# The products of c with the powers of a, on VectorE instead of GpSimd, in a two-block transformer kernel

## The chip, the cores and the metric

The kernel runs on one core of one Trainium2 chip, as one program. The metric is the device time of one execution in microseconds (us); lower is better. The times of several executions of the same program are given by their median.

## The reference

Two transformer blocks are computed on 512 tokens of width 1024, in float32. The first block has, side by side, a chunked attention of 8 heads and a state space mixer, then an attention to 256 memory tokens, then a feed-forward part that picks experts by keys (16384 experts, 8 heads, 16 picks). The second block has a dilated and a differential attention and a second part with experts. The first step of the first block is a projection of the normalised tokens to q, k, v (512 columns each) and u (512 columns).

The change lies in the state space mixer. It works on 32 groups of 16 channels, each with 64 complex states. Cut to what matters:

```
step = exp(log_step);  mag = exp(lr * step)
ar, ai = mag * cos(li * step), mag * sin(li * step)      # one complex a per state
bbr, bbi = (fr + i fi) * (br + i bi)                      # discretised input matrix
bu = einsum('blgc,gpc->blgp', u, bb)
x[l] = a * x[l-1] + bu[l]                                 # associative scan over 512 tokens
y = einsum('blgp,gcp->blgc', xr, cr) - einsum('blgp,gcp->blgc', xi, ci) + d * u
y = gelu(y);  y = y * sigmoid(y @ w_glu + b_glu)
```

## The kernel before

The kernel is a straight-line program without loops on the chip. Each engine has its own queue, which it works off strictly in order and in which it waits for the results of others. The order in a queue is not that of the source: when the program is built, a planner goes through it with estimated durations of its own, and puts next in each queue the instruction that is earliest in the source among those it takes to be ready. So the weight splits and norms of a projection (early lines) stand in VectorE's queue in between the tables of the state space mixer (later lines).

*The projections* (lines 130 to 262). The normalised tokens are transposed and split in a high and a low part, and each weight is split in the same way, so that a product needs three matmuls (mm3, lines 117 to 120). A weight of 128 rows and 512 columns is loaded by SP's queue, cast by ScalarE (L76: the high part) and subtracted by VectorE (L77: the low part). For one projection there are 8 such weights and 4 tiles of 128 tokens, 96 matmuls of 512 columns, which are summed in four PSUM tiles. ScalarE then copies each PSUM tile out (L230), which makes it free for the next projection. For q and k (head_proj, L224) ScalarE squares the copy (L235), VectorE sums the squares by heads (L236), and after the four tiles VectorE makes the inverse root (L57 to L72) and scales (L249), and TensorE transposes (L252). The tile of squares has one buffer, so square 2 waits for sum 1:

```
sq = pool.tile([128, n], F32, name="sq", tag="sq", bufs=1)
A.activation(out=sq, in_=raw[:, t, :], func=AF.Square)
V.tensor_reduce(out=ss[:, t * nh:(t + 1) * nh], in_=sq.rearrange("p (h d) -> p h d", d=hd), axis=AX.X, op=OP.add)
```

The projections come in the order q, k, u, v (L259 to L262). u is written to memory (L214), from where the mixer reads it later.

*The tables of the mixer* (lines 265 to 392). While TensorE works on the projections, VectorE makes from the parameters: a itself (L299 to L302), bbr and bbi (L341), and the powers a^0 to a^8 in par and pai by doubling (L343 to L351). GpSimd copies the powers in reverse order into rar and rai (L355, L356, 16 small copies). Then come the products of c with the powers (L358 to L371): car and cai, each 128 partitions x 16 x 9 x 16, made in two pieces (5 powers, then 4), with three instructions for each piece and each of car and cai, so twelve instructions, six of 1280 and six of 1024 elements on each of 128 partitions. One operand of the multiplications repeats each power 16 times, the other repeats c for each power. Behind them in the source VectorE makes the phase tables phc and phs (L375 to L388): squarings of 128x16 (uc, us) and products of 128x16 to 128x512, with the function cmul (L318 to L332), and dec (L390). GpSimd also clears toep (L373), which has no input and runs first of all.

*Who reads what.* rar, rai, bbr and bbi are read by the gb products (L420), the first VectorE work of the mixer after the projections; their tiles lie in memory that is free when the projections' and the tables' pools have been closed (L392 to L395). car and cai are read by TensorE in L441 and L442, after the gb products, and in L511 and L512. phc, phs and dec are read by the recurrence (L488 to L496). These stages are put in between the heads of the chunked attention (L596 on), by a list of steps written out by hand (L578).

Of the kernel before, what the change touches and what calls it, by code (L numbers as in the profile page):

```python
# [14 lines left out]
OP = mybir.AluOpType  # L15
# [8 lines left out]
def build(tc, I, out, dbg=None, stop=None):  # L24
# [22 lines left out]
    V, A, G, T, S = nc.vector, nc.scalar, nc.gpsimd, nc.tensor, nc.sync  # L47
# [286 lines left out]
    def bc(ap, axis, n):  # L334
        sh = list(ap.shape)
        sh.insert(axis, n)
        return ap.unsqueeze(axis).broadcast_to(sh)
# [26 lines left out]
    for o, n in ((0, 5), (5, 4)):  # L364
        w_ = slice(o, o + n)
        pr_, pi_ = bc(par[:, :, w_], 3, 16), bc(pai[:, :, w_], 3, 16)
        u = st.tile([128, 16, 5, 16], F32, name="cau", tag="cau")[:, :, 0:n]
        for dst, x, y in ((car, cr, nci), (cai, nci, ncr)):
            G.tensor_tensor(out=dst[:, :, w_], in0=pr_, in1=bc(x, 2, n), op=OP.mult)
            G.tensor_tensor(out=u, in0=pi_, in1=bc(y, 2, n), op=OP.mult)  # L370
            G.tensor_tensor(out=dst[:, :, w_], in0=dst[:, :, w_], in1=u, op=OP.add)  # L371
    toep = b1.tile([128, 32, 128], F32, name="toep")
    G.memset(toep, 0.0)  # L373

# [5 lines left out]
    for lvl in range(9):  # L380
        if lvl >= 3:
            n = 1 << (lvl - 3)
# [371 lines left out]
    for h2 in range(2):  # L754
        if h2 == 1:
            ws = keep_w(wk, I["w_mem_o"], 8, 0)
        for t in range(NT):
# [3 lines left out]
            for hh in range(2):  # L761
# [10 lines left out]
                for j in range(2):  # L772
# [3 lines left out]
                            in1=zs.unsqueeze(2).broadcast_to([128, 2, 256]), op=OP.mult)  # L776
# [1102 lines left out]
```

## Time and profile before

| | |
|---|---|
| runs | 3839.08, 3841.64, 3839.0 us; median 3839.08 |
| profiled execution, its own time | 3833.36 us |
| its span in the profile | 3831.6 us |
| mean granted clock of TensorE | 0.981 |
| busy: TensorE, VectorE, ScalarE, GpSimd | 96%, 78%, 43%, 47% of the span |
| chain that ended last: TensorE, VectorE | 71%, 15% of the span |

The profile is that of one execution. Its views give, among others, the busy time of each engine in any stretch, the instructions of each engine in order of time, and who waited for whom. An instruction's row in the view in order of time has its start and its duration in us, the engine (PE is TensorE, DVE is VectorE, ACT is ScalarE, POOL is GpSimd), the line of the source, the operation, the tiles out<-in, the shapes, and in brackets the idle time of the engine before it with what ended that. A duration may reach a little into the next instruction's, since the engine takes the next one while the last results are being written. Spans on GpSimd are rough.

### The profile page before, as it was taken

The numbers are of one execution on the slowest core, as the hardware profiler recorded it, in microseconds if no ns is written. First come the engines' busy times: TensorE is split into PE (matmuls) and PEld (weight loads), VectorE is DVE, ScalarE is ACT, GpSimd is POOL, SyncE is SP. The second block draws the span as 40 slices with busy tenths as digits, with TensorE's granted clock in tenths as the row PEclk, the third lists the DMA queues.
The fourth block names the chain that finished last, engine by engine and source line by source line (L and its number), as shares of the span: only waits on it lengthen the run. The fifth ranks groups of instructions, "written<-read, shape, count | busy, mean of one in ns | idle before, by whom it ended". The sixth has DMA issues, their size and how long they took to land.

```text
span 3831.6 us, 53218 instructions
## 1 busy us (share of the span) xinstructions
PE 3659.9 (96%) x19062; PEld 3158.1 (82%) x19062; DVE 2999.7 (78%) x5554; ACT 1653.4 (43%) x2567; POOL 1802.3 (47%) x1192
## 2 busy tenths in 40 slices
PE   6999999899999999999899999999899999999999
PEld 4767788788899999987777777788888899999987
DVE  8556469996898988878746577689996898888875
ACT  3554433375333333333344588333474333333333
POOL 3000037613778787760324100247424778877740
PEclk8999999999999999999999999999999999999999
DMA  3423132257899999988322333332358999999884
GB/s 111 106 95 121 55 120 88 79 207 263 318 337 321 315 325 326 326 304 281 106 72 69 90 95 103 119 107 82 111 224 269 327 338 327 319 316 325 306 284 147
DMA packets 333515, 789.04 MB, mean 206 GB/s; under 512 B 32433, under 2 KB 152321, under 8 KB 329857
## 3 DMA queue, kind: packets, MB, share of 16 engines
q1 hardware_dynamic: 259520, 517.17, 40.8%
q0 software_dynamic: 73728, 268.47, 19.3%
q8 instruction: 150, 2.46, 0.3%
q14 instruction: 117, 0.95, 0.1%
HBM read 725.34 MB, written 59.01 MB: 205 GB/s over the span
## 4 chain that ended last, share of the span: by engine, by line
PE 71%; DVE 15%; DMA 5%; ACT 4%; issue 3%; POOL 2%; SPq 1%; DVEq 0%; POOLq 0%; ACTq 0%
PE y L1305 8%; PE y L1307 8%; PE y L1306 8%; PE pa L1114 7%; PE pa L1112 7%; PE pa L1111 7%; PE pgg L1213 4%; PE mm L119 3%; PE mm L120 3%; PE mm L118 3%; DVE E L968 2%; ACT stg L1214 2%; PE mt L1603 1%; PE mt L1601 1%; DVE eq L959 1%
## 5 line engine op out<-in xcount | busy, mean ns | idle before, releaser
L1104 POOL TENSOR_TENSOR ul<-ur,uh 128x1024 fp32r<-128x1024 f32 x256 | 695.5, 2717 | 435.6 <-PE pa L1114 261.1
L1111 PE MATMUL pa<-phi,uh 128*128 128x384 f32 x2048 | 698.7, 341 | 0.9 <-ACT ga L1116 0.9
L1112 PE MATMUL pa<-plo,uh 128*128 128x384 f32 x2048 | 696.0, 340 | 0.0
L1305 PE MATMUL y<-vh,wh 128*128 128x512 f32 x1536 | 596.0, 393 | 15.0 <-ACT wh L1274 13.6
L1306 PE MATMUL y<-vl,wh 128*128 128x512 f32 x1536 | 600.4, 392 | 3.6 <-DVE vl L1276 3.5
L1307 PE MATMUL y<-vh,wl 128*128 128x512 f32 x1536 | 601.8, 393 | 2.1 <-DVE wl L1277 2.1
L1276 DVE TENSOR_TENSOR vl<-vr,vh 128x1024 fp32r<-128x1024 f32 x256 | 361.3, 1411 | 215.3 <-ACT vh L1275 215.1
L1274 ACT CAST wh<-w 128x384 fp32r<-128x384 f32 x256 | 131.5, 514 | 755.0 <-PE y L1306 547.7
L1251 DVE SCALAR_TENSOR_TENSOR acc<-vrow,act,acc 128x1024 f32<-128x1024 f32 x256 | 408.9, 1597 | 56.2 <-DMA vrow<-in_peer_v_dram,ei 28.4
L1240 DVE SCALAR_TENSOR_TENSOR urow<-urow,hgat 128x1024 f32<-128x1024 f32 x256 | 408.9, 1604 | 30.4 <-DMA urow<-in_peer_u_dram,ei 15.6
L1114 PE MATMUL pa<-phi,ul 128*128 128x384 f32 x2048 | 403.1, 340 | 15.9 <-POOL ul L1104 15.8
L1098 ACT CAST uh<-ur 128x1024 fp32r<-128x1024 f32 x256 | 269.6, 1053 | 325.4 <-issue 212.6
L1111 PEld LDWEIGHTS pa<-phi,uh 128*128 128x128 f32 x2048 | 389.5, 190 | 9.6 <-ACT ga L1116 1.2
L1112 PEld LDWEIGHTS pa<-plo,uh 128*128 128x128 f32 x2048 | 389.6, 190 | 9.1
L1114 PEld LDWEIGHTS pa<-phi,ul 128*128 128x128 f32 x2048 | 362.4, 190 | 18.0 <-POOL ul L1104 18.0
L1305 PEld LDWEIGHTS y<-vh,wh 128*128 128x128 f32 x1536 | 289.1, 189 | 71.2 <-ACT wh L1274 14.3
L1307 PEld LDWEIGHTS y<-vh,wl 128*128 128x128 f32 x1536 | 289.2, 189 | 68.5 <-DVE wl L1277 5.3
L1306 PEld LDWEIGHTS y<-vl,wh 128*128 128x128 f32 x1536 | 289.5, 189 | 63.4 <-DVE vl L1276 7.4
L77 DVE TENSOR_TENSOR wl<-wr,wh 128x512 fp32r<-128x512 f32 (+1 forms) x276 | 177.9, 653 | 142.4 <-ACT wh L76 142.1
L1275 ACT CAST vh<-vr 128x1024 fp32r<-128x1024 f32 x256 | 267.7, 1046 | 35.6 <-DMA vr<-in_peer_v_dram 24.9
L1273 DVE TENSOR_TENSOR w<-gbuf,ga 128x384 f32<-128x384 f32 x256 | 212.0, 830 | 37.1 <-DMA gbuf<-Gd 36.0
L76 ACT CAST wh<-wr 128x512 fp32r<-128x512 f32 (+1 forms) x276 | 149.4, 550 | 209.3 <-PE mm L120 129.2
(533 smaller groups left out, 7241.0 us busy)
## 6 DMA issues: line engine op xcount, KB each, us to landing
vr<-in_peer_v_dram SPq DMA_DIRECT2D x128, 512.0 KB, 6.3
ur<-in_peer_uT_dram SPq DMA_DIRECT2D x128, 512.0 KB, 4.6
vr<-in_expert_v_dram SPq DMA_DIRECT2D x128, 512.0 KB, 6.4
ur<-in_expert_uT_dram SPq DMA_DIRECT2D x128, 512.0 KB, 4.7
gbuf<-Gd SPq DMA_DIRECT2D x64, 768.0 KB, 8.8
Gd<-stg SPq DMA_DIRECT2D x24, 1920.0 KB, 6.3
wr<-in_w_in_dram SPq DMA_DIRECT2D x104, 256.0 KB, 2.8
war<-in_w_ada_dram SPq DMA_DIRECT2D x48, 512.0 KB, 4.2
```

Source lines behind the costliest of these rows:

```text
L1098: A.copy(out=uh, in_=ua[e])
L1104: G.tensor_tensor(out=ul, in0=raw, in1=uh.bitcast(F32), op=OP.subtract)
L1111: T.matmul(pa, uh[:, k, :], hi[:, k, 0:NDT], start=(k == 0), stop=False)
L1112: T.matmul(pa, uh[:, k, :], lo[:, k, 0:NDT], start=False, stop=False)
L1114: T.matmul(pa, ul[:, k, :], hi[:, k, 0:NDT], start=False, stop=(k == 7))
L1240: V.scalar_tensor_tensor(out=row, in0=row, scalar=1.0, in1=hg_, op0=OP.mult, op1=OP.mult, accum_out=act[:, k:k + 1])
L1251: V.scalar_tensor_tensor(out=acc, in0=rows_.pop((1, k)), scalar=act[:, k:k + 1], in1=acc, op0=OP.mult, op1=OP.add)
L1275: A.copy(out=vh, in_=vr)
L1276: V.tensor_tensor(out=vl, in0=vr, in1=vh.bitcast(F32), op=OP.subtract)
L1305: T.matmul(y[t][c], wh[:, ts], vh[:, cs_], start=(e_ == 0), stop=False)
L1306: T.matmul(y[t][c], wh[:, ts], vl[:, cs_], start=False, stop=False)
L1307: T.matmul(y[t][c], wl[:, ts], vh[:, cs_], start=False, stop=(e_ == 127))
```

## The change

The three instructions in the inner loop are issued to VectorE (V) where they were issued to GpSimd (G). Nothing else in the source differs; the planner orders the queues anew.

```
     for o, n in ((0, 5), (5, 4)):
         w_ = slice(o, o + n)
         pr_, pi_ = bc(par[:, :, w_], 3, 16), bc(pai[:, :, w_], 3, 16)
         u = st.tile([128, 16, 5, 16], F32, name="cau", tag="cau")[:, :, 0:n]
         for dst, x, y in ((car, cr, nci), (cai, nci, ncr)):
-            G.tensor_tensor(out=dst[:, :, w_], in0=pr_, in1=bc(x, 2, n), op=OP.mult)
-            G.tensor_tensor(out=u, in0=pi_, in1=bc(y, 2, n), op=OP.mult)
-            G.tensor_tensor(out=dst[:, :, w_], in0=dst[:, :, w_], in1=u, op=OP.add)
+            V.tensor_tensor(out=dst[:, :, w_], in0=pr_, in1=bc(x, 2, n), op=OP.mult)
+            V.tensor_tensor(out=u, in0=pi_, in1=bc(y, 2, n), op=OP.mult)
+            V.tensor_tensor(out=dst[:, :, w_], in0=dst[:, :, w_], in1=u, op=OP.add)
     toep = b1.tile([128, 32, 128], F32, name="toep")
     G.memset(toep, 0.0)
```

## Rows read from the trace of the kernel before

**Rows 1.** The page, part 1: busy time of each engine.
```profile
PE 3659.9 (96%) x19062; PEld 3158.1 (82%) x19062; DVE 2999.7 (78%) x5554; ACT 1653.4 (43%) x2567; POOL 1802.3 (47%) x1192
```
**Rows 2.** Two stretches: length, PE, PEld, DVE, ACT, POOL busy (instructions), clock, DMA, GB/s.
```profile
45.00:80.00 35.00, 12.69 (x43) 9.55 (x43) 34.73 (x75) 6.68 (x12) 23.36 (x11) 0.67 0.10 26
81.00:116.00 35.00, 34.37 (x159) 28.22 (x158) 22.50 (x55) 14.94 (x26) 0.00 (x0) 1.00 0.29 83
```
**Rows 3.** Waits from 43 to 77 us: in total, times, longest.
```profile
ACT sq L235 <- DVE ssh L236: 24.6, 3, 13.9
...
PE mm L118 <- ACT hraw L230: 17.4, 2, 11.6
```
**Rows 4.** ScalarE in order of time: squares 1 and 2 of q.
```profile
40.35 0.63 ACT L235 ACTIVATE sq<-hraw 128x512 f32<-128x512 f32 x1
...
55.57 0.63 ACT L235 ACTIVATE sq<-hraw 128x512 f32<-128x512 f32 x1 [13.89 <-DVE ssh L236]
```
**Rows 5.** TensorE in order of time: the instructions behind its long idle pieces.
```profile
56.73 0.80 PE L118 MATMUL mm<-wh,hThi 128*128 128x512 f32 x1 [11.60 <-ACT hraw L230]
...
64.21 0.79 PE L118 MATMUL mm<-wh,hThi 128*128 128x512 f32 x1 [5.83 <-ACT hraw L230]
...
76.01 1.94 PE L252 MATMUL ptq<-ident,hraw 128*128 128x128 f32 x8 [4.28 <-issue]
```
**Rows 6.** VectorE in order of time, 43 to 69 us.
```profile
43.08 2.26 DVE L331 TENSOR_TENSOR cm<-uc,us 128x16 f32<-128x16 f32 x1
45.26 0.16 DVE L327 TENSOR_TENSOR uc<-uc 128x16 f32<-128x16 f32 x1
45.37 2.33 DVE L332 TENSOR_TENSOR us<-us,cm 128x16 f32<-128x16 f32 x1
...
54.81 0.67 DVE L236 TENSOR_REDUCE ssh<-sq 128x8 f32<-128x512 f32 x1
...
66.31 2.42 DVE L327 TENSOR_TENSOR phc<-phc,uc 128x32 f32<-128x32 f32 x1
```
**Rows 7.** GpSimd in order of time: the first of the twelve products, and the third.
```profile
35.70 2.39 POOL L369 TENSOR_TENSOR car<-par,ssm_cr 128x1280 f32<-128x1280 f32 x1
...
45.27 2.40 POOL L369 TENSOR_TENSOR cai<-par,nci 128x1280 f32<-128x1280 f32 x1
```
**Rows 8.** The stretch with eleven of the products: GpSimd busy, then VectorE busy.
```profile
42.80:68.80 26.00, 25.56 (x12) 0.67 0.03 10
...
42.80:68.80 26.00, 25.76 (x27) 0.67 0.03 10
```
**Rows 9.** VectorE by line and form: count, busy us, mean ns, idle before.
```profile
L328 DVE TENSOR_TENSOR cm<-gin,phs 128x1024 f32<-128x1024 f32 x1 | 1.2, 1218 | 0.0
...
L328 DVE TENSOR_TENSOR cm<-rai,bbi 128x512 f32<-128x512 f32 x2 | 1.4, 688 | 0.0
```
**Rows 10.** VectorE in order of time: a split, and sums 1 and 2 of k.
```profile
37.62 1.03 DVE L77 TENSOR_TENSOR wl<-wr,wh 128x512 fp32r<-128x512 f32 x1 [1.85 <-ACT wh L76]
...
92.26 0.69 DVE L236 TENSOR_REDUCE ssh<-sq 128x8 f32<-128x512 f32 x1
93.71 0.69 DVE L236 TENSOR_REDUCE ssh<-sq 128x8 f32<-128x512 f32 x1 [0.76 <-ACT sq L235]
```
**Rows 11.** VectorE in order of time: the last phase table product, the first gb product.
```profile
91.57 0.68 DVE L332 TENSOR_TENSOR phs<-phs,cm 128x512 f32<-128x512 f32 x1
...
125.56 0.69 DVE L327 TENSOR_TENSOR gb<-rar,bbr 128x512 f32<-128x512 f32 x1 [1.32 <-DMA ud<-ut]
```
**Rows 12.** Two longer stretches, columns as in rows 2.
```profile
35.00:143.00 108.00, 84.77 (x369) 68.42 (x368) 75.64 (x170) 37.69 (x66) 31.55 (x23) 0.89 0.29 87
...
143.00:200.00 57.00, 50.90 (x308) 37.49 (x307) 30.07 (x87) 30.70 (x78) 0.58 (x4) 0.88 0.37 77
```
**Rows 13.** In order of time: three copies on GpSimd, a split on VectorE.
```profile
41.84 1.08 POOL L356 COPY rai<-pai 128x16 f32<-128x16 f32 x3
...
41.84 0.68 DVE L77 TENSOR_TENSOR wl<-wr,wh 128x512 fp32r<-128x512 f32 x1
```

More of the change, by code (lines that the diff above doesn't have):

```diff
@@ L368, in build @@
         for dst, x, y in ((car, cr, nci), (cai, nci, ncr)):
-            G.tensor_tensor(out=dst[:, :, w_], in0=pr_, in1=bc(x, 2, n), op=OP.mult)
-            G.tensor_tensor(out=u, in0=pi_, in1=bc(y, 2, n), op=OP.mult)
-            G.tensor_tensor(out=dst[:, :, w_], in0=dst[:, :, w_], in1=u, op=OP.add)
+            V.tensor_tensor(out=dst[:, :, w_], in0=pr_, in1=bc(x, 2, n), op=OP.mult)
+            V.tensor_tensor(out=u, in0=pi_, in1=bc(y, 2, n), op=OP.mult)
+            V.tensor_tensor(out=dst[:, :, w_], in0=dst[:, :, w_], in1=u, op=OP.add)
     toep = b1.tile([128, 32, 128], F32, name="toep")
```

## The prediction

> **What bounds the kernel now.** I read the page first, then the same 35 us of two neighbouring projections with the busy time of each engine, then the waits in the bad one, then the engines' instructions in order of time.
>
> The page says that TensorE is busy for 3659.9 us, 96% of the span [rows 1]. So only a stretch in which TensorE stands still can give much, and the products of c sit in one, near the start. From 45 to 80 us TensorE runs 43 matmuls; from 81 to 116 us, in work of the same kind, 159 in the same 35 us [rows 2]. Its granted clock is 0.67 in the first stretch, a mix of the two levels of 1.2 and 2.4 GHz, and 1.00 in the second. GpSimd is busy for 23.36 us of the first and not at all in the second.
>
> The waits name the chain [rows 3]: TensorE waits 17.4 us in two pieces for ScalarE's copies of the finished q tiles (L230), which free the PSUM tiles for the k projection; ScalarE waits 24.6 us for VectorE's sums of squares (L236), since the tile of squares has one buffer. On ScalarE, square 2 starts at 55.57 after 13.89 us of idling and only then comes copy 3 [rows 4]. TensorE's own long idle pieces are 11.60, 5.83 and 4.28 us, 21.7 us together [rows 5].
>
> Why are the sums late? VectorE stands in front of them with phase table products of 128x16 elements. Such an instruction takes 0.16 us when nothing is in its way; from 43.08 us on eleven of them take some 2 us each, the first 2.26 and the last (128x32) 2.42 us [rows 6]. They end where a GpSimd product ends: VectorE's 45.37 + 2.33 is 47.70, GpSimd's 45.27 + 2.40 is 47.67 [rows 6, 7]. The sum L236 reads one tensor and takes 0.67 us in the middle of this, as long as in a stretch without GpSimd (0.69) [rows 6, 10]. So the sums are late because two-input VectorE instructions ahead of them are held, not because VectorE has that much to do.
>
> **The change, part by part.**
>
> *Removed from GpSimd:* twelve products, the first at 35.70 us [rows 7] of 2.39 us, the other eleven filling 25.56 of the 26 us from 42.8 to 68.8 [rows 8]; 28 us. GpSimd then has nothing to do from 81 to 116 us [rows 2], so its own time is worth nothing. What counts is the hold that goes: in those 26 us VectorE has 25.76 us busy in 27 instructions [rows 8], of which two sums at 0.67 and 25 small ones at about 0.17 make 5.6; some 20 us is holding.
>
> *What that gives TensorE.* At the pace of the undisturbed stretch, 159 in 35 us, 43 matmuls take 9.5 us, so the stretch loses 25.5 us [rows 2]: 21.7 us of idling in the long pieces and 3.8 us in short ones and at the low clock after them. Of the 43, 16 are short transposes, in two pieces of eight of which one is shown [rows 5]. If these took no time at all, the other 27 would need 5.9 us and the loss would be 29.1 us; that is the far bound. I take 25.5, since the second stretch has transposes too.
>
> *Added to VectorE:* the twelve products. VectorE has no 128x1280 product in this trace. The bounds are the 128x1024 one (1.218 us, same type) and, on the far side, GpSimd's 2.4 us. The VectorE row is nearer, and the step from 512 elements (0.688 us, with operands broadcast in the same way) to 1024 costs 0.53 us, so 1280 should take 1.48 us [rows 9]. Six at 1.22 and six at 1.48 make 16.2 us. At 2.4 us each for the long ones it would be 21.7 us.
>
> *What of it lies on the path.* The products come earlier in the program than the phase tables (L380 on) and later than the projections' sums and splits. They now take the place in VectorE's queue that held phase table work had: a sum that becomes ready can stand behind a product in progress, at most 1.48 us. TensorE needs two of the four q sums: sum 1 releases copy 3, sum 2 copy 4. In the undisturbed projection sums follow one another at 1.45 us [rows 10] and TensorE is busy for 34.37 of 35 us [rows 2]. So the likely cost is two products' time less some slack: between 0 and 3.0 us, of which I take 2.5, because the order is fixed before the run and will not hit the free moments. The far bound is all twelve ahead of the sums, 16.2 us. Behind a waiting sum on ScalarE stand the next copy and the next weight cast; behind those TensorE.
>
> *Before 45 us* the last q weights can be held by a product as well. VectorE stood idle for 1.85 us there, waiting for a cast [rows 10], which covers one product and costs nothing; without that cover it costs 1.2 us.
>
> *The phase tables move back.* They end at 92.25 us, with the last of their products. With 20 us of holding gone and 16.2 us added they end near 88 us. Their reader, the first gb product, starts at 125.56 behind a transfer of u [rows 11], and that moves to about 103. Cover 14 us: cost nothing. VectorE as a whole was busy 75.64 of 108 us from 35 to 143 us [rows 12]; less 20, plus 16.2 is 72 us in about 85. It is fuller, but not full.
>
> *GpSimd's copies stay* (L355, L356). Three of them took 1.08 us, while a VectorE split with two inputs beside them took 0.68 us [rows 13], no longer than 512 elements take elsewhere [rows 9]: there VectorE did not pay. Their results are read at 103 us, so I count 0. The Trainium skill, page SBUF — State Buffer, section "Who interferes with whom", says that issue order decides which of the two is blocked, and for the whole instruction. By that rule some of the products would stand behind a copy; no row here shows VectorE paying for one. At a third of 1.08 us for each of twelve products an estimate by that rule is 4.3 us more on VectorE, and 3820 if all of it were on the path.
>
> No transfer is moved, added or removed, and SP's queue keeps its order; its weight loads come earlier with TensorE.
>
> *After 81 us* TensorE hardly stops [rows 2], so what is won stays won through the projections, and the later stages hang on their results.
>
> **Sum.** 25.5 - 2.5 = 23 us. The profiled execution took 3833.36, so 3810.4 for its like; it lies 5.7 us under the median of the three runs. Against the median: 3839.08 - 23.0 = 3816.
>
> **The rivals.**
>
> *B, the products stand in front of the sums.* If the planned order puts all twelve ahead of sum 1, as they are ready at the same time, 16.2 us replace the hold: 25.5 - 16.2 = 9.3 us won, 3830. For it: the first GpSimd product started at 35.70 and the first square was done at 40.35 + 0.63 us [rows 4, 7], and several products fit between. Against it: twelve do not, and the sums are earlier in the program.
>
> *C, won and given back.* TensorE arrives at the attention stage 23 us sooner and waits there for the recurrence's tables or for transfers that do not move. Under 7.7 us would be left, so 3832 to 3840. For it: TensorE already has gaps there, 6.1 us of the 57 after 143 [rows 12]. Against it: the tables have 14 us of cover and the transfers of u start from TensorE's results.
>
> *D, slower: the late sums have another cause.* The place is sum 1 at 54.81. If its lateness came from the one tile of squares and the planned order rather than from the hold, the loss would stay and the products would be added in front of the sums: 3839.08 + 16.2 = 3855. It decides if sum 1 starts after 54.81 and sum 4 after 70. Against it: square 1 was done at 40.98 and VectorE had mostly small work between it and the sum [rows 4, 6].
>
> *E, the change does not do what it says:* the hold stays because of the copies. It would then be at most the copies' own time, as counted above; I give it no chance apart from C.
>
> **How the numbers follow.** The forecast, 3816, has 0.75; B 0.13; C 0.07; D 0.05. A measurement of this kernel can tell about 0.2%, 7.7 us, from no change; the forecast and B are both faster than that, C is within, D is slower: 0.88, 0.07, 0.05. The range reaches up to B, 3830. Downwards it takes the far bound of the loss with nothing paid: 3839.1 - 29.1 = 3810.
>
> **What would show it.** Right: the twelve lines L369 to L371 on VectorE at 1.22 and 1.48 us; none of the 128x16 products over 0.3 us; sum 1 before 46 us; TensorE's idling between 45 and 60 us under 4 us and its clock at 1.00; the first gb product near 103. Wrong: sum 1 later than 50 us (B); TensorE idling for 15 us more than now after the projections (C); a VectorE instruction still held for 2 us (D or E).

## The result, and the profile after

The changed kernel takes 3806.59 us (median of 7 runs, 3801.29 to 3822.07); the kernel before, run in turn with it, 3832.39 us (7 runs, 3826.77 to 3841.64, the three of the table above among them). The ratio is 0.993, with a 95% interval from 0.9916 to 0.9944. The profiled execution took 3806.59 us, with a span of 3804.6. The forecast had the sign and the main mechanism, the hold, right. Its time, 3839.08 - 23.0 = 3816.1, was 9.5 us too high, and the range, which began at 3810, missed the result by 3.4 us. By these medians the gain is 25.8 us, and the interval of the ratio lets it be anything from 21.5 to 32.2; its size is therefore read from places in the trace, below.

The page of the changed kernel, part 1, answers to [rows 1]:

```profile
PE 3652.2 (96%) x19062; PEld 3153.4 (83%) x19062; DVE 3005.2 (79%) x5566; ACT 1653.4 (43%) x2567; POOL 1775.5 (47%) x1180
```

Twelve instructions went from GpSimd (1192 to 1180) to VectorE (5554 to 5566). Nothing else was added or removed. VectorE's busy time up to the last copy of v falls from 101.0 us (in 142.0) to 92.4 (in 115.5), although 16 us of products were added: the holding had counted as busy. That its total on the page rises by 5.5 us comes from the part behind the mixer, 14.2 us more there with the same 5060 instructions.

The stretches of [rows 2] in the changed kernel (length, then busy time of PE, PEld, DVE, ACT, POOL with counts, clock, DMA share, GB/s):

```profile
45.00:80.00 35.00, 33.61 (x162) 27.24 (x161) 34.60 (x109) 17.25 (x30) 0.00 (x0) 1.00 0.33 90
81.00:116.00 35.00, 34.53 (x154) 27.90 (x152) 21.26 (x51) 13.37 (x24) 0.96 (x1) 1.00 0.45 143
```

TensorE now runs 162 matmuls from 45 to 80 us instead of 43, at a granted clock of 1.00 instead of 0.67. VectorE is as full as before (34.60 of 35 us), but with 109 instructions instead of 75. At 162 in 35 us, the 43 of before take 9.3 us, so some 25.7 us were won in this stretch.

VectorE in order of time, against [rows 6]:

```profile
35.15 1.48 DVE L369 TENSOR_TENSOR car<-par,ssm_cr 128x1280 f32<-128x1280 f32 x1
37.08 1.36 DVE L77 TENSOR_TENSOR wl<-wr,wh 128x512 fp32r<-128x512 f32 x2 [0.45 <-ACT wh L76]
...
38.76 1.49 DVE L370 TENSOR_TENSOR cau<-pai,nci 128x1280 f32<-128x1280 f32 x1
...
40.94 1.50 DVE L371 TENSOR_TENSOR car<-car,cau 128x1280 f32<-128x1280 f32 x1
42.36 0.67 DVE L236 TENSOR_REDUCE ssh<-sq 128x8 f32<-128x512 f32 x1
...
48.28 0.67 DVE L236 TENSOR_REDUCE ssh<-sq 128x8 f32<-128x512 f32 x1
```

Sum 1 starts at 42.36 us instead of 54.81, and sum 4 at 48.28. A product of 1280 elements takes 1.48 to 1.50 us and one of 1024 takes 1.22 us, as forecast.

ScalarE in order of time, against [rows 4]:

```profile
39.85 0.63 ACT L235 ACTIVATE sq<-hraw 128x512 f32<-128x512 f32 x1
40.59 0.59 ACT L230 COPY hraw<-mm 128x512 f32<-128x512 f32 x1
41.95 0.59 ACT L230 COPY hraw<-mm 128x512 f32<-128x512 f32 x1 [0.77 <-PE mm L120]
43.12 0.63 ACT L235 ACTIVATE sq<-hraw 128x512 f32<-128x512 f32 x1 [0.58 <-DVE ssh L236]
```

Here the order changed as well: copy 3 (41.95) now stands ahead of square 2 (43.12); before, it stood behind it [rows 4]. The planner put it there. Copy 3 therefore no longer depends on sum 1 at all, and the idle time in front of it was ended by TensorE.

All of TensorE's waits from 45 to 117 us, against [rows 3]:

```profile
PE ptq L252 <- issue: 1.0, 1, 1.0
PE mm L118 <- ACT ut L213: 0.4, 1, 0.4
PE ptq L252 <- DVE hraw L249: 0.4, 1, 0.4
```

Where it stays won: the last copy of v (L262, the end of the projections) starts at 115.5 us instead of 142.0, 26.5 us sooner. The mixer's output is written (L521) at 270.3 instead of 295.4, 25.1 us sooner. From there to the end the two spans have 3534.3 and 3536.2 us left. The profiled executions differ by 26.8 us (3833.36 and 3806.59), so the gain is made ahead of the last copy of v and nearly all of it kept.

### The profile page after: what moved, and what is told of

Read it like the earlier page. It is cut to its first block, busy times and chain, and to the rows that moved or that the text cites. A ratio compares the mean times of both kernels' runs of the same rounds, so it can differ in the third digit from the quotient of the medians.

```text
span 3804.6 us, 53216 instructions
## 1 busy us (share of the span) xinstructions
PE 3652.2 (96%) x19062; PEld 3153.4 (83%) x19062; DVE 3005.2 (79%) x5566; ACT 1653.4 (43%) x2567; POOL 1775.5 (47%) x1180
## 4 chain that ended last, share of the span: by engine, by line
PE 70%; DVE 16%; DMA 5%; ACT 4%; issue 3%; POOL 2%; SPq 1%; DVEq 0%; ACTq 0%; POOLq 0%
PE y L1305 8%; PE y L1307 8%; PE y L1306 8%; PE pa L1114 7%; PE pa L1112 7%; PE pa L1111 7%; PE pgg L1213 4%; PE mm L119 3%; PE mm L118 3%; PE mm L120 3%; DVE E L968 2%; ACT stg L1214 2%; DMA vrow<-in_peer_v_dram,ei 1%; DVE eq L959 1%; PE mt L1603 1%
## 5 line engine op out<-in xcount | busy, mean ns | idle before, releaser
L1273 DVE TENSOR_TENSOR w<-gbuf,ga 128x384 f32<-128x384 f32 x256 | 221.2, 866 | 38.1 <-DMA gbuf<-Gd 18.7
```

## The experiments

Two places measure each run below: the last copy of v (115.5 after, 142.0 before) and the write of the mixer's output (270.3 and 295.4). They lie ahead of the long rest of the kernel, whose length differs between runs by more than most of the effects. Each run has one trace. In the two traces of the kernel before, the last copy of v differs by 0.2 us and the mixer's output by 2.8 us (295.4 and 298.2), so smaller differences at the second place say nothing.

**The kernel before, as a run of its own.** No edit.

> The kernel before once more, for its own level: the three runs first shown had a median of 3839, later ones lay lower. If the level is 3832 to 3836, the forecast's base was 4 to 7 us too high and its difference of 23 us is to be judged against that; if it is 3839, the difference was mis-sized by 9 us or more. The trace should have the end of the projections at 142 us and the mixer's output at 295 us, as in the first trace.

Measured: 3835.97 us (12 runs, 3829.1 to 3848.52), ratio 0.9998 (0.9988 to 1.0009) to 23 runs of the same kernel with a median of 3835.48. The 22 runs beside the first experiments have 3835.86. Single runs go from 3826.56 to 3848.52. The profiled one, the longest at 3848.52, had its last copy of v at 141.8, as in the first trace, and its mixer's output at 298.2; 3548.5 us of its span lie behind the mixer's output, 12 more than in the run profiled first. So the level of the kernel before is near 3836. The three runs at 3839.0 to 3841.64 agreed with each other and were still some 3 us high.

**GpSimd kept at work on like products.** The products stay on VectorE, and GpSimd makes twelve like them into a tile that nobody reads.

```
             V.tensor_tensor(out=dst[:, :, w_], in0=dst[:, :, w_], in1=u, op=OP.add)
+            g = st.tile([128, 16, 5, 16], F32, name="gdm", tag="gdm")[:, :, 0:n]
+            for _ in range(3):
+                G.tensor_tensor(out=g, in0=pr_, in1=bc(x, 2, n), op=OP.mult)
```

> The changed kernel, products on VectorE, with twelve products of the same sizes made on GpSimd as well, into a tile that nobody reads. Theory, the hold: two-input VectorE instructions after 36 us last 2 us or more again and end with GpSimd's, the sums are late, and at least the 26 us are lost again: 3832 or more, up to 3850, since VectorE's own twelve are now held too. Rival, the gain came from another order of the queues or from the tables moving back behind the products: the order is the changed kernel's, so 3806.

Measured: 3831.28 us (10 runs), ratio 0.9989 (0.9977 to 1.0002), just under the 3832 or more of the theory and far from the rival's 3806; last copy of v at 139.3. The stretch from 45 to 80 us (columns as above), and VectorE in it:

```profile
45.00:80.00 35.00, 21.28 (x76) 15.42 (x74) 35.00 (x25) 7.75 (x14) 34.22 (x18) 0.78 0.18 45
```

```profile
54.38 2.38 DVE L57 TENSOR_SCALAR rhv<-ssh 128x32 f32<-128x32 f32 x1
56.68 1.48 DVE L371 TENSOR_TENSOR cai<-cai,cau 128x1280 f32<-128x1280 f32 x1
...
64.37 1.94 DVE L70 TENSOR_TENSOR rht<-rhy 128x32 f32<-128x32 f32 x1
```

GpSimd beside it:

```profile
53.99 9.29 POOL L374 TENSOR_TENSOR gdm<-par,nci 128x1280 f32<-128x1280 f32 x3
```

With work on GpSimd that nobody waits for, the gain is gone. VectorE gets through 25 instructions instead of 109. An instruction on 128x32 takes 1.93 to 2.38 us; without GpSimd beside it the same L57 takes 0.17 us. GpSimd pays as well: three of its products take 9.29 us, 3.1 us each, where one took about 2.4 us before [rows 7]. VectorE has the work of the changed kernel here and no more, and from the first product on the instructions of VectorE, ScalarE and TensorE come in the changed kernel's order, one for one; so all that is lost is lost to what GpSimd does beside it. This shows the hold as the cause, rules out the new order of the queues, and shows that the gain comes from GpSimd's silence, not from VectorE being the faster maker of the products.

**GpSimd kept at work that only writes.** Instead of products, eight memsets of toep, put in the same place by one copy that waits for the powers.

```
     toep = b1.tile([128, 32, 128], F32, name="toep")
-    G.memset(toep, 0.0)
+    G.tensor_copy(out=toep[:, 0, 0:16], in_=pai[:, :, 8])
+    for _ in range(8):
+        G.memset(toep, 0.0)
```

> The changed kernel with GpSimd busy for 28 us from about 43 us on with eight memsets of 128x4096, which write and read nothing (they clear toep, eight times over). Theory, the hold by reads of two-input instructions: no VectorE instruction is stretched, 3806. Rival, any work on GpSimd slows VectorE: small products last 3.5 us again and the time is 3825 or more.

Measured: 3817.34 us (7 runs), ratio 0.9951 (0.9936 to 0.9965); last copy of v at 124.4. Neither expectation held: the time lies between the two. GpSimd, then VectorE:

```profile
44.92 28.59 POOL L375 MEMSET toep<- 128x4096 f32 x8
```

```profile
46.66 1.48 DVE L370 TENSOR_TENSOR cau<-pai,ncr 128x1280 f32<-128x1280 f32 x1
...
49.25 2.83 DVE L57 TENSOR_SCALAR rhv<-ssh 128x32 f32<-128x32 f32 x1
49.34 2.75 DVE L371 TENSOR_TENSOR cai<-cai,cau 128x1280 f32<-128x1280 f32 x1
52.12 3.55 DVE L59 TENSOR_SCALAR rhh<-rhv 128x32 int32<-128x32 int32 x1
...
59.40 1.22 DVE L370 TENSOR_TENSOR cau<-pai,nci 128x1024 f32<-128x1024 f32 x1
```

The two-input products run beside the memsets at their full pace (1.48 and 1.22 us). The one-input instructions L57, L59 and L61 are held, 2.83 to 3.55 us instead of 0.17. They end where a memset ends: 44.92 + 2 x 28.59 / 8 is 52.07, and L57 ends at 52.08. Three two-input instructions have long rows too, 2.75 to 3.46 us; each is the one directly behind L57, L59 or L61 and ends within 0.01 us of it, as L371 does (49.34 + 2.75). The Trainium skill, page SBUF — State Buffer, section "Who interferes with whom", says of the first kind that a VectorE instruction with two inputs contends with a GpSimd instruction that reads, not with one that only writes, and counts tensor_scalar among those that can contend with GpSimd if their operands meet certain conditions. The trace agrees, with these numbers. So it is not GpSimd's being busy that costs, but what its instructions do and which VectorE instructions fall beside them. Three held instructions still cost 9 us at the projections.

**Memsets of half the size**, to shorten each hold: sixteen memsets, on the two halves of toep in turn.

```
+    G.tensor_copy(out=toep[:, 0, 0:16], in_=pai[:, :, 8])
+    G.tensor_copy(out=toep[:, 16, 0:16], in_=pai[:, :, 8])
+    for _ in range(8):
+        G.memset(toep[:, 0:16, :], 0.0)
+        G.memset(toep[:, 16:32, :], 0.0)
```

> The run with eight memsets on GpSimd again, now as sixteen of half the size (64 KB less each per piece, 1.8 us). There, VectorE's one-input tensor_scalar instructions (L57, L59, L61 of the q norm) lasted 2.8 to 3.6 us, to the end of a memset, and the two-input products did not. Theory, each of the three waits for the end of one memset: they now last 1.9 us at most, and the stage ends 4 to 5 us after the changed kernel's instead of 8.8. Rival, the loss goes by GpSimd's busy time of 28 us: 8 to 9 us again.

Measured: 3834.96 us (10 runs), ratio 1.0002 (0.999 to 1.0014); last copy of v at 140.5. Both expectations fail. GpSimd's last two memsets, then VectorE:

```profile
70.11 1.82 POOL L376 MEMSET toep<- 128x2048 f32 x1
71.86 1.82 POOL L377 MEMSET toep<- 128x2048 f32 x1
```

```profile
49.94 23.77 DVE L57 TENSOR_SCALAR rhv<-ssh 128x32 f32<-128x32 f32 x1
50.03 23.68 DVE L371 TENSOR_TENSOR cai<-cai,cau 128x1280 f32<-128x1280 f32 x1
```

L57 ends at 73.71 us, the last memset at 73.68: one small instruction, taken up during the third memset, stood past the ends of thirteen of them and got in only at the last, and the product behind it ended with it. The memsets' rows take 1.82 us and start 1.75 us apart, so by the rows each begins 0.07 us before the one ahead of it has ended. (Half of toep is 1 MB; the 64 KB of the expectation is a slip.)

**Memsets of the same size, all on one half.** As before, but sixteen times the first half (the second half once).

```
+    G.tensor_copy(out=toep[:, 0, 0:16], in_=pai[:, :, 8])
+    G.memset(toep[:, 16:32, :], 0.0)
+    for _ in range(16):
+        G.memset(toep[:, 0:16, :], 0.0)
```

> The changed kernel, with one copy that fixes the place, one memset of the second half of toep and then sixteen memsets of its first half, 128x2048 each: the sizes of the run with alternating halves, but each one writes what the one before it wrote. There the small one-input instruction L57 lasted 23.77 us, to the end of the last memset; with eight memsets of the whole tile, each over the one before, such instructions lasted 2.8 to 3.6 us, to the end of one memset. Theory 1, the next memset is taken up while the last one is still writing when they write different places, so that the hold never ends: here every memset writes the same place, the hold ends at each, L57 lasts at most 1.9 us and the projections end before 126 us. Theory 2, short memsets follow one another too quickly whatever they write: L57 lasts over 15 us again, and the projections end near 140 us. If memsets of the same half also start 1.75 us apart with rows of 1.82 us and L57 still gets through at one of the first two ends, neither overlap nor size is the reason.

Measured: 3808.45 us in one run, beside one of 3829.61 of the kernel before; last copy of v at 119.2.

```profile
45.33 29.86 POOL L376 MEMSET toep<- 128x2048 f32 x16
```

The same sixteen by their line (shortest, median and longest in ns, first and last start in us), then the eight of the whole tile:

```profile
L376 POOL MEMSET toep<- x16: 1805/1812/1823, 45.3 to 73.4; 128x2048 f32 x16
```

```profile
L375 POOL MEMSET toep<- x8: 3512/3524/3537, 44.9 to 70.0; 128x4096 f32 x8
```

VectorE:

```profile
49.66 1.28 DVE L57 TENSOR_SCALAR rhv<-ssh 128x32 f32<-128x32 f32 x1
...
51.15 1.66 DVE L59 TENSOR_SCALAR rhh<-rhv 128x32 int32<-128x32 int32 x1
...
52.85 1.84 DVE L61 TENSOR_SCALAR rhy<-rhh 128x32 int32<-128x32 int32 x1
```

Theory 1 gave these numbers. The memsets start 1.87 us apart (29.86 / 16), and the held instructions end where the third, fourth and fifth have passed (45.33 + 3 x 1.87 is 50.94, as is 49.66 + 1.28). The size is the same as before; what differs is that each memset writes what the last one wrote. A row of one takes 1.81 us here and took 1.82 there, but here some 0.06 us lie between one and the next, where those on alternating places began 0.07 us before the last had ended. The eight memsets of the whole tile, each over the last, have such gaps too: their rows take 3.52 us and start 3.59 us apart. With a gap VectorE is let in at the next end; without one it was let in only at the last. That the gap is what lets it in fits all three runs, but place and gap go together in them, and a few hundredths of a microsecond are read from spans that are rough; so this reason is argued, not shown.

**Every product made twice on VectorE**, to find the room it has.

```
-        for dst, x, y in ((car, cr, nci), (cai, nci, ncr)):
+        for dst, x, y in ((car, cr, nci), (car, cr, nci), (cai, nci, ncr), (cai, nci, ncr)):
```

> The changed kernel with each of the twelve products made twice on VectorE (the same values written again), 16 us more of VectorE. Theory, the hold: VectorE had 15 us of idling between 35 and 117 us and the sums wait for at most one product each, so the stage ends within 5 us of the changed kernel's and the time is 3806 to 3812. Rival, the products' own time counts (case B of the prediction): the second twelve stand in front of the sums and splits, 16 us later, about 3823.

Measured: 3813.8 us (4 runs), ratio 0.9937 (0.9914 to 0.9959); last copy of v at 115.7, so another 16 us of products cost the projections nothing, as the theory had it. But its 3806 to 3812 was missed by 1.8 us, and the mixer's output is written at 283.4, 13 us later than in the changed kernel. The two profiled spans differ by the same 13 us (3817.6 and 3804.6). VectorE at the end of the phase tables, here and then in the changed kernel:

```profile
112.71 0.69 DVE L332 TENSOR_TENSOR phs<-phs,cm 128x512 f32<-128x512 f32 x1
113.49 0.69 DVE L327 TENSOR_TENSOR gb<-rar,bbr 128x512 f32<-128x512 f32 x1
```

```profile
91.64 0.69 DVE L332 TENSOR_TENSOR phs<-phs,cm 128x512 f32<-128x512 f32 x1
...
98.63 0.69 DVE L327 TENSOR_TENSOR gb<-rar,bbr 128x512 f32<-128x512 f32 x1 [0.82 <-DMA ud<-ut]
```

In the changed kernel the first gb product waits for the transfer of u, 6.3 us after the tables (91.64 + 0.69 is 92.33). With twice the products it stands directly behind the tables, 14.9 us later. The room is in the tables' deadline, and 16 us more are too much for it. The median of the four runs shows less of this than the place does: 3813.8 lies within the changed kernel's spread.

**Four tiles for the squares, products on GpSimd**, to take the one tile of squares out of the chain while the hold stays.

```
-            sq = pool.tile([128, n], F32, name="sq", tag="sq", bufs=1)
+            sq = pool.tile([128, n], F32, name="sq", tag="sq", bufs=4 if W is Win else 1)
```

> The kernel before, products on GpSimd, with four tiles of squares instead of one in the q and k projections. Theory: the chain from held sums to TensorE goes through the one tile of squares; with four, ScalarE copies q tiles 3 and 4 out without waiting for a sum, TensorE's two pieces of 17.4 us go though VectorE is held as before, and only the late q transposes (4.3 us) and late splits of weights stay: 12 to 20 us faster than before. Rival, the held splits of the k weights stop TensorE as soon as the copies do not: under 8 us faster.

Measured: 3834.45 us (10 runs), ratio 0.9995 (0.9985 to 1.0005); last copy of v at 142.0. The theory failed and the rival held. ScalarE's third and fourth copies run at once, at 41.96 and 43.63 us, but TensorE now stops for 20.62 us in one piece, where it had stopped for 17.4 us in two [rows 3]. TensorE, then VectorE:

```profile
69.57 0.80 PE L119 MATMUL mm<-wl,hThi 128*128 128x512 f32 x1 [20.62 <-DVE wl L77]
```

```profile
65.88 2.34 DVE L327 TENSOR_TENSOR phc<-phc,uc 128x32 f32<-128x32 f32 x1
...
68.84 0.67 DVE L77 TENSOR_TENSOR wl<-wr,wh 128x512 fp32r<-128x512 f32 x1
```

The split that it waits for stands on VectorE behind the held phase table products and starts at 68.84. The chain through the tile of squares [rows 3, 4] was only the first of the links that led to VectorE's queue. Taking it out brings up the next one, the split of a weight, with the same end.

**The products on GpSimd, but later**, at a time when VectorE has less to do: a small copy of the finished k into each destination makes eleven of the twelve wait.

```
         for dst, x, y in ((car, cr, nci), (cai, nci, ncr)):
+            G.tensor_copy(out=dst[:, 0, o, :], in_=kT[:, 0, 496:512])
             G.tensor_tensor(out=dst[:, :, w_], in0=pr_, in1=bc(x, 2, n), op=OP.mult)
```

> The kernel before, products on GpSimd, but eleven of the twelve wait until the k projection is evacuated (four small copies from kT ahead of them), so that they fall beside the u and v projections. Theory, it matters what stands behind the held instructions: at that time VectorE has no q sums to make, the phase tables are nearly done, and the splits it makes are of weights three ahead of TensorE. VectorE's two-input instructions last 2 us or more beside them, but the stage ends within 5 us of the changed kernel's 116 us; 3805 to 3815 by the trace. Rival, a held VectorE costs TensorE the same wherever it falls: the stage ends near 140 us as before, no gain.

Measured: 3820.71 us (4 runs), ratio 0.996 (0.9944 to 0.9976); last copy of v at 122.2, mixer's output at 286.5. Both expectations failed: the theory's 3805 to 3815 and 5 us, by 5.7 and 1.2 us, and the rival's 140 us by far. VectorE beside the products, which now run from 82.13 to 110.7 us, and the last product:

```profile
85.69 2.21 DVE L77 TENSOR_TENSOR wl<-wr,wh 128x512 fp32r<-128x512 f32 x1 [0.61 <-ACT wh L76]
...
98.98 7.42 DVE L77 TENSOR_TENSOR wl<-wr,wh 128x512 fp32r<-128x512 f32 x3 [5.36 <-ACT wh L76]
...
110.73 0.69 DVE L327 TENSOR_TENSOR gb<-rar,bbr 128x512 f32<-128x512 f32 x1 [4.33 <-DMA bglu<-in_ssm_b_glu_dram]
```

```profile
108.30 2.40 POOL L372 TENSOR_TENSOR cai<-cai,cau 128x1024 f32<-128x1024 f32 x1
```

By the time, the same GpSimd work costs about half as much here, without any of it going to VectorE; at the projections it costs 7 us instead of 26.5. A split takes 2.1 to 2.6 us instead of 0.68, but few instructions stand behind it: the cost of a hold is what queues behind the held instruction. At the mixer's output 16 us of the changed kernel's gain are missing, since the first gb product now comes at 110.73. That need not be a hold: the product starts 0.03 us after the last GpSimd product has ended (108.30 + 2.40), though the profile puts its wait down to a transfer (bglu). Which of the two let it go is not shown.

**One more product off GpSimd.** On top of the change, the gate products of the mixer (L696), which stand on the chain of waits of the changed kernel (1.74 us at 293.90), are made by VectorE as well.

```
-        G.tensor_tensor(out=gl, in0=gl, in1=yt[:, t, :], op=OP.mult)
+        V.tensor_tensor(out=gl, in0=gl, in1=yt[:, t, :], op=OP.mult)
```

> The changed kernel with GpSimd's other products of the mixer moved to VectorE as well: the four of the gate (L696, 128x512, 1.5 us each on GpSimd, one of them on the chain at 294 us). Theory: VectorE makes one in 0.69 us and each of the two pairs lies on the way to a norm; 1 to 4 us faster than the changed kernel in the stretch from 285 to 320 us, too little to be seen in the time. Rival, VectorE's queue delays other work there: 0 to 3 us slower.

Measured: 3805.01 us (6 runs, 3800.75 to 3812.23), ratio 0.9926 (0.9912 to 0.9939). From 285 to 320 us TensorE is busy for 32.69 us instead of 29.71, and a pair of these products takes 1.30 us instead of 2.98. The mixer's output, ahead of these products, was already 1.3 us early (269.0), so not all of the difference in the stretch is theirs. The median is the lowest of all, but the two intervals lie over one another nearly whole: the run can't be told from the change alone.

## Why the prediction was right, and where it was wrong

*The hold: right.* That VectorE's small two-input instructions are held, and the sums only stand behind them, is what GpSimd's products beside an otherwise changed kernel bring back. No phase table product of 128x16 lasts over 0.20 us in the changed kernel, where eleven had taken some 2 us [rows 6]. The part that the prediction did not see: it read the tile of squares as the way from VectorE to TensorE. The run with four tiles shows that this link was not needed: a second way from VectorE's queue, the split of a weight, was as late.

*The loss of 25.5 us: right.* The stretch gave 25.7 us, the end of the projections 26.5.

*The price on VectorE: right.* 1.48 us from the step between two shorter rows, measured 1.48 to 1.50; 1.22 as in [rows 9].

*The 2.5 us of products in front of the sums: the term that was mis-sized.* Measured near 0. Sum 1 did stand behind a product: its square was done at 39.85 + 0.63 = 40.48, the product L371 took 1.50 us from 40.94, and the sum started at 42.36. The step took the order of ScalarE for given, with copy 3 behind square 2. The new order has copy 3 ahead, so TensorE did not pay. TensorE's only waits from 45 to 80 us are two of those above, 1.0 us at the transposes of q and 0.4 us at those of k. The end of 0 in the step's own bounds was the right one.

*"Against the median: 3839.08 - 23.0 = 3816": the step that failed.* It rested the time on three runs and let the profiled execution's 3833.36 stand 5.7 us under them as an oddity. Some sixty later runs put the kernel before near 3836, and the runs in turn with the change had a median of 3832.39. Against that median the miss of 9.5 us is 6.7 of base and 2.8 of gain (23.0 forecast, 25.8 measured). Against the later level it divides so: 3.6 from this base (3839.08 to 3835.5), 3.8 from the size of the gain (23.0 to the 26.8 between the two profiled executions), and the rest, 2.1, lies within the spread of runs. The same step fixed the low end of the range: 3810 allowed for the largest gain but for no doubt of the base. The sum against the profiled execution, 3810.4, was nearer, but 3.8 us too high as well; most of that is the 2.5 us above and the 1 us by which the end of the projections gained more than the 25.5 of the forecast.

*Before 45 us: right.* The first product, at 35.15, took the place of VectorE's idling; the split behind it waits for 0.45 us instead of 1.85 [rows 10].

*The phase tables: the size off, the answer right.* Forecast to end near 88 us, with gb near 103 and 14 us between them; measured 92.33, 98.63 and 6.3. The sum took off the hold and added the products, but not that splits and norms of the next projections come sooner too and stand in the same queue, 109 instructions in the stretch for 75. The cover was enough; the run with double products shows where it ends.

*GpSimd's copies: right at 0.* GpSimd in the changed kernel:

```profile
35.29 1.56 POOL L356 COPY rai<-pai 128x16 f32<-128x16 f32 x2
38.90 2.19 POOL L355 COPY rar<-par 128x16 f32<-128x16 f32 x3 [2.05 <-DVE par L329]
```

Both groups start 0.14 us behind a product on VectorE (35.15 and 38.76) and are held by it, to 2.19 us for three copies against the 1.08 of [rows 13]; the product keeps its 1.48 to 1.49 us. The rule of the Trainium skill that the prediction cited (page SBUF — State Buffer, section "Who interferes with whom": issue order decides, for the whole instruction) agrees with this. The estimate of 4.3 us by it put the wrong engine second.

*The rivals.* B did not come: seven of the products were still to come when sum 4 was done. D fell: sum 1 came at 42.36 us, sum 4 at 48.28, where it needed 54.81 and 70. C did not come either (25.1 of 26.5 us still stand at the mixer's output), but its mechanism is real: it took 13 us in the run with double products. E did not come: no VectorE instruction was held in the stretch.

## What to carry to other kernels

Long two-input instructions on a spare GpSimd were not free here. Before placing them there, look at which VectorE instructions run beside them, and at what stands behind those in its queue; a tiny instruction that lasts 2 us and ends with a GpSimd instruction is the sign. Removing one link between the held queue and TensorE gains nothing when other links lead to the same queue: remove the hold, or, for part of the gain, move it to where little queues behind it. A forecast to 0.3% needs a base from many runs; where the profiled execution and a few runs differ, work from both and let the range hold both.

## What the runs showed of the hardware that was not expected

Memsets on GpSimd, which read nothing, left VectorE's two-input products at 1.22 and 1.48 us, except some directly behind a held instruction, and held one-input instructions on 128x32 to a memset's end, 1.3 to 3.6 us instead of 0.17. Sixteen memsets of 1.82 us on two places in turn held one such instruction for 23.77 us, past the ends of thirteen of them; sixteen on one place let it in at the next end. The Trainium skill's page SBUF — State Buffer (section "Who interferes with whom") gives the shared ports to the engine that issues first, for its whole instruction, while the other is blocked. A block past the ends of thirteen instructions goes beyond what that sentence says, and here the measurement decides.
